# Gate and up by seven block products instead of eight (Strassen) in a mixed mLSTM and attention block

## The chip, the cores and the metric

The kernel runs on one core of a Trainium2 chip. The metric is the time of one execution on the device in microseconds (us), the median of several runs. All times below are of the kernel before the change, unless said otherwise.

## The reference, cut to what matters

```python
SEQ = 512
D_MODEL = 1024
D_FF = ((8 * D_MODEL + 3 * 256 - 1) // (3 * 256)) * 256          # 2816
...
        mod = jnp.dot(c_act, ada_w[l]) + ada_b[l]
        sh1, sc1, g1, sh2, sc2, g2 = jnp.split(mod, N_MOD, axis=-1)
...
        merged = (jax.nn.sigmoid(ga) * jnp.einsum('bsm,md->bsd', ym, p_mlstm[l])
                  + jax.nn.sigmoid(gb) * jnp.einsum('bsa,ad->bsd', ya, p_moba[l]))
        x = x + g1[:, None, :] * jnp.einsum('bsd,de->bse', merged, w_out[l])

        h = modulate(rms_norm(x, norm2_g[l]), sh2, sc2)
        f = jax.nn.silu(jnp.einsum('bsd,df->bsf', h, w_gate[l])) * jnp.einsum('bsd,df->bsf', h, w_up[l])
        x = x + g2[:, None, :] * jnp.einsum('bsf,fd->bsd', f, w_down[l])
    return rms_norm(x, normf_g)
```

All tensors are float32. The change touches the product of h (512 tokens x 1024) with w_gate and w_up (each 1024 x 2816); batch and depth are 1. ym and ya, the outputs of the mLSTM and of the attention, are computed ahead of what is shown.

## The kernel before, in words

**Products in float32.** Each float32 operand is held as two rounded parts, hi and lo. `mm3` (L220 to L223) makes one 128-deep product as three matmuls: hi by hi, hi by lo, lo by hi.

**Weights.** They come in 68 numbered blocks, the *chunks*, of mostly 1024 x 256 numbers (1 MB), kept in a buffer `raw` of four (`load`, L151). The attention and mLSTM input chunks come first, then C_P = 27 to 30 (merge projection), C_OUT = 31 to 34 (w_out), C_GU = 35 to 56 (w_gate and w_up in turn, 256 columns of D_FF each) and C_DN = 57 to 67 (w_down). `cvt(n, half)` turns half a chunk into hi (ACT, L204) and lo (DVE, L206), in `whl`. The chunks C_OUT and C_DN are first multiplied by the gate rows g1 or g2 on DVE (`gate_weights`, L176). `begin(n)` issues the load of a chunk two or three ahead and converts the first half of the next; `mid(n)` the second half.

**Gate and up.** Activations lie transposed: h2 is eight hi/lo pairs of 128 x 512 (128 of the 1024 features, 512 tokens). A unit is 128 columns of D_FF: eight steps of `mm3` on a chunk's 128 x 128 pieces (stationary) with h2 (512 columns, moving), so 24 matmuls of N = 512 a unit and 48 a chunk. `glu` takes silu of the gate unit on ACT (L1371) and multiplies by the up unit on DVE (L1372). The very first pair of chunks (`first`) runs in two halves of 256 tokens, since the second half of h2 is not there yet.

**Background jobs.** The rows of `mod` come from 24 jobs j, numbered over 256-column pieces of ada_w: an `ada` load of 1 MB in the buffers that the chunks use too, 15 operations on GpSimd (L271, L274), and a one-matmul `finish` (L743) with an addition on DVE (L745) that puts the piece into its row. Jobs 20 to 23 make g2. `rows_free` holds the jobs 20 to 23 back: they start once something has been appended to it. A recording layer with an estimated clock (`spend`, `pooled`) decides at build time where the pieces of a job stand between the other instructions; every engine then runs its own instructions in the order of that record.

**Queues.** All loads of chunks, of `ada` and of x are issued by SP, in one order. A load whose buffer is not free holds up those behind it.

Of the kernel before, what the change touches and what calls it, by code (L numbers as in the profile page):

```python
# [19 lines left out]
NT = 4  # L20
# [79 lines left out]
def block_kernel(ctx, tc, x, wall, adaw, pcol, prow, positions, inv_freq, out):  # L100
# [80 lines left out]
    def cvt(n, half, what=None, eng=None):  # L181
        if n >= len(KS):
            return
        if n not in parts:
            both = wp.tile([128, 2 * RAW], F32R, tag="whl", name=nm("whl"))
            parts[n] = (both[:, :SIZES[n]], both[:, SIZES[n]:2 * SIZES[n]])
        hi, lo = parts[n]
        if n == C_MV:
            dst = [t.rearrange("p (k n) -> p k n", k=8) for t in (hi, lo)]
            src = raws[n][:, :2048].rearrange("p (k n) -> p k n", k=8)  # L190
            ks = slice(half * 4, half * 4 + 4)
            cuts = [(src[:, ks, :], ks, slice(8, 264))]
# [27 lines left out]
    def mm3(o, lh, ll, rh, rl, start, stop):  # L220
        PE.matmul(o, lh, rh, start=start, stop=False)  # L221
        PE.matmul(o, lh, rl, start=False, stop=False)  # L222
        PE.matmul(o, ll, rh, start=False, stop=stop)  # L223
# [1074 lines left out]
    def h2_part(hf, qs):  # L1298
        for q in qs:
            pb = bank("a")  # L1300
            hq = T()
            for kk in range(2):
                k = 2 * q + kk
                for e in range(2):
                    PE.transpose(pb[:, kk * 256 + e * 128:kk * 256 + e * 128 + 128],
                                 nrm[2 * hf + e][k // 4][:, blk(k % 4)], ident[:])
            for kk in range(2):
                k = 2 * q + kk
                hm = hq[:, kk * 256:kk * 256 + 256]
                hi, lo = (h2[k][e][:, hf * 256:hf * 256 + 256] for e in range(2))  # L1310
# [84 lines left out]
    glu(bs[0], bs[2])
    glu(bs[1], bs[3])
    hT = h2
    rows_free.append(1)
    nfrow = []
# [7 lines left out]
    for ci in range(1, NF // 2):
        c = C_GU + 2 * ci
        cg = begin(c)
        pg = [None, None]  # L1410
        pg[0] = unit(cg, 0, bank("m"))
        mid(c)
        pg[1] = unit(cg, 1, bank("m"))
        cu = begin(c + 1)
        if ci == NF // 2 - 1:
            fps.update({k: fsplit(k) for k in range(2)})
        glu(pg[0], unit(cu, 0, bank("b")))
        mid(c + 1)
        glu(pg[1], unit(cu, 1, bank("b")))
        if ci == 4:  # L1420
            nfrow += [W(), W()]
            for q in range(2):
                SP.dma_start(nfrow[q][:, :512], flat(prow, PB + 2 * D + q * 512, [[0, 128], [1, 512]]))
# [146 lines left out]
```

## Time and profile before

| | us |
|---|---|
| median of three runs | 789.71 (789.25 to 789.99) |
| the profiled execution's own time | 789.44 |
| its span | 787.6 |
| TensorE matmul (PE) busy | 776.9, 99% |
| VectorE (DVE) busy | 416.4, 53% |
| ScalarE (ACT) busy | 311.4, 40% |

The span runs from the first to the last instruction of the profiled execution. An engine is busy while it works on at least one instruction; what follows is read by stages, since an average over the span hides which engine is the limit where. The stages of interest here: merge projection until 371.2 us, w_out until 416.5, the first gate and up pair until 441, the other 20 gate and up chunks until about 660, then w_down.

### The profile page before, as it was taken

Reading aid. Unit: us, or ns where it says so; the run is one execution under the profiler, and the core shown is the slowest. Engines: PE = TensorE matmul, PEld = TensorE weight load, DVE = VectorE, ACT = ScalarE, POOL = GpSimd, SP = SyncE. Lnnn points to the kernel's source line nnn. Section 1 sums busy time; section 2 is a strip of 40 time slices with the busy share of each in tenths; the row PEclk is TensorE's granted clock in tenths of the full one; section 3 lists DMA queues with packets and bytes.
Section 4 is the critical chain, followed back from the end, with each engine's and each line's share of the span. In section 5 each row is a group of like instructions: output and inputs, shape, how many; then the busy total and the mean of one; then the engine's idle time right before and its main releaser. Section 6 shows DMA issues by size and latency. Waiting matters only on the chain.

```text
span 787.6 us, 10146 instructions
## 1 busy us (share of the span) xinstructions
PE 776.9 (99%) x3891; PEld 642.3 (82%) x3891; DVE 416.4 (53%) x671; ACT 311.4 (40%) x541; POOL 299.5 (38%) x423
## 2 busy tenths in 40 slices
PE   8999999999999999999999999999999999999996
PEld 7789888778887787788889888888888888888885
DVE  4768687665565543478646333322322246555565
ACT  6679653324454454322356322221222113332243
POOL 5574436999866878950003695000000000000000
PEclk9999999999999999999999999999999999999999
DMA  9953325345431432345223425532232332222002
GB/s 326 387 195 142 107 80 174 120 150 205 155 108 54 161 107 107 134 187 183 102 90 108 154 74 200 213 108 75 86 107 108 107 108 88 76 104 107 0 1 107
DMA packets 22960, 102.49 MB, mean 130 GB/s; under 512 B 3448, under 2 KB 3584, under 8 KB 13312
## 3 DMA queue, kind: packets, MB, share of 16 engines
q1 hardware_dynamic: 21088, 99.43, 34.7%
q10 hardware_dynamic: 1824, 2.43, 1.1%
q8 instruction: 30, 0.49, 0.3%
q14 instruction: 18, 0.15, 0.1%
HBM read 97.65 MB, written 2.10 MB: 127 GB/s over the span
## 4 chain that ended last, share of the span: by engine, by line
PE 92%; DVE 3%; ACT 1%; DMA 1%; POOL 1%; issue 1%; POOLq 0%; ACTq 0%; DVEq 0%
PE psm L221 15%; PE psm L223 14%; PE psm L222 14%; PE psb L221 10%; PE psb L223 10%; PE psb L222 10%; PE psa L221 2%; PE psa L223 2%; PE psa L222 2%; PE psa L1091 1%; PE psc L1149 1%; PE psb L489 1%; PE psb L1132 1%; PE psa L591 1%; PE psm L591 1%
## 5 line engine op out<-in xcount | busy, mean ns | idle before, releaser
L206 DVE TENSOR_TENSOR whl<-raw,whl 128x1024 fp32r<-128x1024 f32 (+3 forms) x125 | 159.1, 1282 | 166.6 <-ACT whl L204 166.5
L204 ACT CAST whl<-raw 128x1024 fp32r<-128x1024 f32 (+2 forms) x124 | 127.2, 1045 | 276.0 <-PE psb L223 158.9
L1472 POOL TENSOR_TENSOR t<-x,v 128x512 f32<-128x512 f32 x1 | 1.3, 1297 | 288.4 <-DVE ss L1478 288.4
L274 POOL TENSOR_TENSOR accp<-accp,prod 128x256 f32<-128x256 f32 x112 | 90.2, 805 | 9.3
L221 PE MATMUL psb<-t,whl 128*128 128x512 f32 (+1 forms) x224 | 84.4, 377 | 0.0
L221 PE MATMUL psm<-t,whl 128*128 128x512 f32 (+1 forms) x224 | 84.3, 377 | 0.0
L223 PE MATMUL psm<-t,whl 128*128 128x512 f32 (+1 forms) x224 | 83.8, 374 | 0.0
L223 PE MATMUL psb<-t,whl 128*128 128x512 f32 (+1 forms) x224 | 83.8, 374 | 0.0
L222 PE MATMUL psm<-t,whl 128*128 128x512 f32 (+1 forms) x224 | 83.7, 374 | 0.0
L222 PE MATMUL psb<-t,whl 128*128 128x512 f32 (+1 forms) x224 | 83.7, 374 | 0.0
L221 PE MATMUL psm<-hh,whl 128*128 128x512 f32 x192 | 77.5, 404 | 0.4 <-ACT x L1073 0.4
L223 PE MATMUL psm<-hh,whl 128*128 128x512 f32 x192 | 75.0, 391 | 0.0
L222 PE MATMUL psm<-hl,whl 128*128 128x512 f32 x192 | 74.9, 390 | 0.0
L271 POOL TENSOR_SCALAR prod<-ada,cact 128x256 f32<-128x256 f32 x112 | 73.9, 660 | 0.0
L223 PEld LDWEIGHTS psm<-t,whl 128*128 128x128 f32 x224 | 42.2, 188 | 7.6
L223 PEld LDWEIGHTS psb<-t,whl 128*128 128x128 f32 x224 | 42.2, 188 | 7.6
L221 PEld LDWEIGHTS psm<-t,whl 128*128 128x128 f32 x224 | 42.2, 188 | 7.4
L222 PEld LDWEIGHTS psm<-t,whl 128*128 128x128 f32 x224 | 42.2, 188 | 7.4
L221 PEld LDWEIGHTS psb<-t,whl 128*128 128x128 f32 x224 | 42.2, 188 | 7.4
L222 PEld LDWEIGHTS psb<-t,whl 128*128 128x128 f32 x224 | 42.2, 188 | 7.4
L223 PEld LDWEIGHTS psm<-hh,whl 128*128 128x128 f32 x192 | 36.0, 188 | 8.2 <-DVE whl L206 0.4
L221 PEld LDWEIGHTS psm<-hh,whl 128*128 128x128 f32 x192 | 36.1, 188 | 8.1 <-ACT x L1073 0.7
(379 smaller groups left out, 1558.2 us busy)
## 6 DMA issues: line engine op xcount, KB each, us to landing
raw<-in_dram SPq DMA_DIRECT2D x59, 1024.0 KB, 4.8
ada<-in_dram SPq DMA_DIRECT2D x16, 1024.0 KB, 4.8
t<-in_dram SPq DMA_DIRECT2D x30, 256.0 KB, 6.1
raw<-in_dram SPq DMA_DIRECT2D x8, 448.0 KB, 6.6
xin<-in_dram SPq DMA_DIRECT2D x4, 512.0 KB, 5.0
v<-in_dram SPq DMA_DIRECT2D x8, 256.0 KB, 5.8
t<-t ACTq DMA_DIRECT2D x32, 64.0 KB, 2.1
x<-in_dram SPq DMA_DIRECT2D x8, 256.0 KB, 7.5
```

The lines of the kernel that those rows point to most:

```text
L204: (eng.tensor_copy if eng else A.copy)(hi[:, s], raws[n][:, s])
L206: (eng or V).tensor_tensor(out=lo[:, s], in0=raws[n][:, s], in1=hi[:, s].bitcast(F32), op=ALU.subtract)
L221: PE.matmul(o, lh, rh, start=start, stop=False)
L222: PE.matmul(o, lh, rl, start=False, stop=False)
L223: PE.matmul(o, ll, rh, start=False, stop=stop)
L271: G.tensor_scalar(t[:], rv[:, k, :], cact[:, k:k + 1], 1.0, op0=ALU.mult, op1=ALU.mult)
L274: G.tensor_tensor(out=p[:], in0=p[:], in1=t[:], op=ALU.add)
L489: PE.matmul(wb[:, :128], ident[:], ones, start=True, stop=True)
L591: PE.matmul(g1[m][:], w[:, blk(m)], h[:], start=k == 0 and e == 0, stop=k == KD - 1 and e == 2)
L1091: PE.matmul(bs[e][:, o:o + n], qp[a][r, blk(i)], kp[b][r, :n], start=g == 0, stop=g == 2)
L1132: PE.transpose(tb[:, o + (i - j) * 128:o + (i - j + 1) * 128], es[i][:, blk(j)], ident[:])
L1149: PE.matmul(yb[e * 64:e * 64 + 64, 128 * j:512], av[j][:, (2 * p + e) * 64:(2 * p + e + 1) * 64], t[j], start=j == 0, stop=j == NT - 1)
```

## The change

Chunks 35 and 36 are computed as before. Chunk 37 is computed in two halves of 256 tokens (`plain`). The 19 chunks 38 to 56 go through `seven`: a chunk's weights are cut in 2 x 2 blocks (512 features x 128 columns), h in 2 x 2 blocks (512 features x 256 tokens), and the four output blocks come from seven products of sums and differences (the form of Strassen's method with common sums, after Winograd) instead of eight. A product is 12 matmuls of N = 256, so a chunk has 84. The sums of h (`moving`) are made once. Those of the weights (`sums13`, `sums24`) are made for each chunk on DVE, in place in `raw`; each is rounded on ACT and its remainder made on DVE (`rounded`, `remainder`). Products 1, 6, 7 and 4 are added up in one PSUM region y, which ACT or DVE reads in between; 5 and 3 in z; 2 in x. Product 4 of a chunk runs after product 1 of the next one.

So that there is room in SBUF, the converted chunks lie in four single slots instead of two double ones, h2 is laid out otherwise, x (the residual, 2 MB) is written to DRAM before the stage and read again after it, and chunks of the merge stage are loaded two ahead rather than three. `rows_free` gets its entry in the merge stage (d == 1) instead of after the first `glu`.

```diff
@@ converted chunks, loads ahead @@
+    def slot():
+        return wp.tile([128, RAW], F32R, tag="whl", name=nm("whl"), bufs=4)
...
-            both = wp.tile([128, 2 * RAW], F32R, tag="whl", name=nm("whl"))
-            parts[n] = (both[:, :SIZES[n]], both[:, SIZES[n]:2 * SIZES[n]])
+            parts[n] = tuple(slot()[:, :SIZES[n]] for _ in range(2))
...
     def begin(n):
-        for e in range(2, 3 if C_MV <= n < C_P - 1 else 4):
+        for e in range(2, 3 if C_MV <= n < C_OUT else 4):
             load(n + e)
@@ merge stage @@
             split(pr[0][:], pr[1][:], ga)
+            if d == 1:
+                rows_free.append(1)
@@ gate and up @@
+    def moving():
+        b = {(r, c): [h2[c][2 * r + j][0] for j in range(2)] for r in range(2) for c in range(2)}
+        u1, u2, u3, u4 = ([H() for _ in range(2)] for _ in range(4))
+        mv.update({1: [p[1:] for p in h2[0][:2]], 2: [p[1:] for p in h2[0][2:]], 3: [p[1:] for p in h2[1][2:]]})
+        for n, o, x0, x1 in ((5, u1, b[0, 1], b[0, 0]), (6, u2, b[1, 1], u1), (7, u3, b[1, 1], b[0, 1]), (4, u4, b[1, 0], u2)):
+            for j in range(2):
+                V.tensor_tensor(out=o[j][:], in0=x0[j][:], in1=x1[j][:], op=ALU.subtract)
...
+    def sums13(n):
+        s1t[n] = T()
+        V.tensor_tensor(out=four(s1t[n]), in0=block(n, 1, 0), in1=block(n, 1, 1), op=ALU.add)
+        V.tensor_tensor(out=block(n, 1, 0), in0=block(n, 0, 0), in1=block(n, 1, 0), op=ALU.subtract)
+
+    def sums24(n):
+        V.tensor_tensor(out=block(n, 0, 0), in0=four(s1t[n]), in1=block(n, 0, 0), op=ALU.subtract)
+        V.tensor_tensor(out=block(n, 0, 1), in0=block(n, 0, 1), in1=block(n, 0, 0), op=ALU.subtract)
+
+    def make(n, products):
+        remainder(*rounded(n, products))
...
+        A.copy(hi, src)
...
+    def remainder(hi, lo, src):
+        V.tensor_tensor(out=lo, in0=src, in1=hi.bitcast(F32), op=ALU.subtract)
+
+    FIRST, LAST = C_GU + 3, C_DN - 1
...
+            mm3(o, wh[:, k, :], wl[:, k, :], hh, hl, k == 0 and p in (1, 2, 5), k == 3, True)
...
+    def late(n):
+        c = at[n]
+        if c["up"]:
+            f0, f1 = c["f"]
+            t0, c22 = c["late"]
+            V.tensor_tensor(out=f0[:], in0=f0[:], in1=t0[:], op=ALU.mult)
+            V.tensor_tensor(out=f1[:, 256:512], in0=f1[:, 256:512], in1=c22, op=ALU.mult)
+
+    def finish4(n):
+        product(n, 4)
+        c = at[n]
+        f = c["f"][1][:, 0:256]
+        if c["up"]:
+            V.tensor_tensor(out=f, in0=f, in1=c["y"], op=ALU.mult)
+        else:
+            A.activation(f, c["y"], AF.Silu)
+
+    def seven(n):
...
+        product(n, 1)
+        A.copy(m1, c["y"])
+        if n > FIRST:
+            finish4(n - 1)
+        elif more:
+            sums13(n + 1)
+        make(n, (7, 4))
+        load(n + 3)
...
+        product(n, 5)
+        A.copy(m5, c["z"])
+        if more:
+            make(n + 1, (5,))
+        product(n, 2)
+        V.tensor_tensor(out=t0[:, 0:256], in0=c["x"], in1=m1, op=ALU.add)
+        if n > FIRST:
+            late(n - 1)
+        if more:
+            make(n + 1, (1, 2))
+        else:
+            cvt(C_DN, 0)
+        product(n, 6)
+        A.copy(u2, c["y"])
+        if more:
+            sums24(n + 1)
+        product(n, 3)
+        if more:
+            six = rounded(n + 1, (6, 3))
+        V.tensor_tensor(out=t0[:, 256:512], in0=c["z"], in1=u2, op=ALU.add)
...
+        product(n, 7)
+        V.tensor_tensor(out=c22, in0=c["y"], in1=m5, op=ALU.add)
...
+        if n + 1 < LAST:
+            sums13(n + 2)
+        if more:
+            remainder(*six)
...
+    for n in range(FIRST, LAST + 1):
+        seven(n)
+    cvt(C_DN, 1)
+    fps[1] = fsplit(1)
+    finish4(LAST)
+    late(LAST)
```

SP's queue in the merge and w_out stages, before: job 19's load (ada_3563) is the last `ada` load; raw_3626, raw_3710, raw_3806, raw_3898 and raw_3960 are chunks 31 to 35, and the eight x loads (seven left out here) stand ahead of the last three.

```order
L264 DMA ada_3563<-in_dram 128x2048 [waits DMAHW0_49,Pool_49]
L159 DMA raw_3626<-in_dram 128x2048 [waits DMAHW6_49,DVE_49]
L159 DMA raw_3710<-in_dram 128x2048 [waits DMAHW7_49,DVE_49]
L1253 DMA x_3754<-in_dram 128x512 [waits PE_49]
...
L159 DMA raw_3806<-in_dram 128x2048 [waits DMAHW5_49,DVE_49]
L159 DMA raw_3898<-in_dram 128x2048 [waits DMAHW6_49,DVE_49]
L159 DMA raw_3960<-in_dram 128x2048 [waits DMAHW7_49,DVE_49]
```

The same place after: ada_3592, ada_3762, ada_3875 and ada_3983 are the loads of jobs 20 to 23, raw_3655 to raw_4066 chunks 30 to 35; v_3764 is a row of ada_b for g2.

```order
L267 DMA ada_3592<-in_dram 128x2048 [waits DMAHW5_49,Pool_49]
L163 DMA raw_3655<-in_dram 128x2048 [waits DMAHW7_49,Pool_49]
L163 DMA raw_3740<-in_dram 128x2048 [waits DMAHW6_49,DVE_49]
L267 DMA ada_3762<-in_dram 128x2048 [waits DMAHW1_49,Pool_49]
L777 DMA v_3764<-in_dram 128x512 [waits PE_49]
L1258 DMA x_3800<-in_dram 128x512
...
L163 DMA raw_3864<-in_dram 128x2048 [waits DMAHW6_49]
L267 DMA ada_3875<-in_dram 128x2048 [waits DMAHW7_49,Pool_49]
L163 DMA raw_3969<-in_dram 128x2048 [waits DMAHW0_49,DVE_49]
L163 DMA raw_3971<-in_dram 128x2048 [waits DMAHW7_49,DMAHW1_49,Pool_49]
L267 DMA ada_3983<-in_dram 128x2048 [waits DMAHW2_49,DVE_49]
```

The `ada` loads of jobs 20 to 23 have moved between the chunk loads of the w_out stage, and ada_3762, ada_3875 and raw_3971 wait on GpSimd (Pool), so whatever stands behind them in SP's queue waits for a job too.

DVE in the gate and up stage, before, one pair of chunks (whl: remainders of weights, 1024 elements a partition; f: the product with the gate unit).

```order
L206 TENSOR_TENSOR whl_5029<-raw_4907,whl_5029 128x1024
L1372 TENSOR_TENSOR f_5057<-f_5057,psb_5032 128x512
L206 TENSOR_TENSOR whl_5029<-raw_4907,whl_5029 128x1024
L1372 TENSOR_TENSOR f_5087<-f_5087,psb_5062 128x512
L206 TENSOR_TENSOR whl_5096<-raw_4970,whl_5096 128x1024 x2
```

The same engine after, one chunk (in the next one stand two further rows, the multiplications of `late`). L1453 are remainders, L1432 to L1437 sums of weights, L1515, L1529 and L1533 additions from PSUM, L1478 the last multiplication of the chunk before.

```order
L1453 TENSOR_TENSOR whl_5581<-t_5527,whl_5581 128x512
L1515 TENSOR_TENSOR t_5534<-psm_5533,v_5535 128x256
L1453 TENSOR_TENSOR whl_5597<-raw_5329,whl_5597 128x1024
L1436 TENSOR_TENSOR raw_5329<-t_5527,raw_5329 128x4x128
L1437 TENSOR_TENSOR raw_5329<-raw_5329 128x4x128
L1529 TENSOR_TENSOR t_5534<-psb_5532,x_5536 128x256
L1533 TENSOR_TENSOR x_5536<-psm_5531,v_5535 128x256
L1432 TENSOR_TENSOR t_5643<-raw_5446 128x512
L1433 TENSOR_TENSOR raw_5446<-raw_5446 128x4x128
L1453 TENSOR_TENSOR whl_5627<-raw_5329,whl_5627 128x1024
L1478 TENSOR_TENSOR hs_5414<-hs_5414,psm_5531 128x256
L1453 TENSOR_TENSOR whl_5680<-raw_5329,whl_5680 128x1024
```

Where a pair of chunks had six operations on DVE, it now has twenty-five: eleven a chunk, and three multiplications a pair (one of them the L1478 above).

## Rows read from the trace of the kernel before

**Rows 1.** The page: busy time of each engine; the chain that ended last.
```profile
PE 776.9 (99%) x3891; PEld 642.3 (82%) x3891; DVE 416.4 (53%) x671; ACT 311.4 (40%) x541; POOL 299.5 (38%) x423
...
PE 92%; DVE 3%; ACT 1%; DMA 1%; POOL 1%; issue 1%; POOLq 0%; ACTq 0%; DVEq 0%
```

**Rows 2.** Busy time by stage: w_out, first pair, most of the others.
```profile
core 0: us, PE busy (x) PEld busy (x) DVE busy (x) ACT busy (x) POOL busy (x), PEclk, DMA share, GB/s
371.20:416.50 45.30, 45.30 (x209) 37.68 (x208) 26.78 (x38) 19.85 (x35) 2.42 (x3) 1.00 0.27 94
416.50:441.00 24.50, 24.50 (x207) 24.46 (x206) 11.97 (x24) 15.98 (x28) 11.97 (x16) 1.00 0.24 86
441.00:650.00 209.00, 209.00 (x925) 173.05 (x925) 64.47 (x66) 46.84 (x56) 34.90 (x50) 1.00 0.35 126
```

**Rows 3.** Timeline of PE, gate and up: start, duration; 31 matmuls, first and last.
```profile
464.69 0.39 PE L223 MATMUL psm<-t,whl 128*128 128x512 f32 x1
...
471.49 0.39 PE L223 MATMUL psm<-t,whl 128*128 128x512 f32 x1
```

**Rows 4.** Timeline of PE, first pair: 49 matmuls of N = 256, first and last.
```profile
416.53 0.28 PE L221 MATMUL psm<-t,whl 128*128 128x256 f32 x1
...
422.29 0.28 PE L221 MATMUL psb<-t,whl 128*128 128x256 f32 x1
```

**Rows 5.** Timeline of DVE, gate and up; in brackets the idle time before.
```profile
525.08 0.69 DVE L1372 TENSOR_TENSOR f<-f,psb 128x512 f32<-128x512 f32 x1 [3.20 <-PE psb L223]
525.69 1.22 DVE L206 TENSOR_TENSOR whl<-raw,whl 128x1024 fp32r<-128x1024 f32 x1
...
531.54 2.36 DVE L206 TENSOR_TENSOR whl<-raw,whl 128x1024 fp32r<-128x1024 f32 x2 [0.32 <-ACT whl L204]
```

**Rows 6.** Groups of DVE by form: busy us, mean ns of one, idle before.
```profile
L198 DVE TENSOR_TENSOR whl<-raw,whl 128x1024 fp32r<-128x1024 f32 x2 | 2.4, 1222 | 1.3 <-ACT whl L196 1.3
...
L903 DVE TENSOR_TENSOR v<-psm,bt 128x256 f32<-128x256 f32 x4 | 1.7, 413 | 0.0
```

**Rows 7.** Groups of ACT by form, the same columns.
```profile
L204 ACT CAST whl<-raw 128x1024 fp32r<-128x1024 f32 x115 | 118.3, 1049 | 270.7 <-PE psb L223 158.9 <-PE psm L223 89.8 <-issue 7.7
...
L1371 ACT ACTIVATE f<-psm 128x512 f32<-128x512 f32 x16 | 9.4, 594 | 0.0
...
L303 ACT COPY t<-psc 128x256 f32<-128x256 f32 x3 | 1.1, 373 | 3.7 <-PE psc L301 3.7
```

**Rows 8.** Timeline of GpSimd: first and last operation of job 19.
```profile
332.68 0.49 POOL L271 TENSOR_SCALAR accp<-ada,cact 128x256 f32<-128x256 f32 x1
...
345.58 0.74 POOL L274 TENSOR_TENSOR accp<-accp,prod 128x256 f32<-128x256 f32 x1
```

**Rows 9.** The same of job 23, in gate and up.
```profile
477.08 0.69 POOL L271 TENSOR_SCALAR accp<-ada,cact 128x256 f32<-128x256 f32 x1 [4.24 <-DMA ada<-in_dram]
...
486.96 0.73 POOL L274 TENSOR_TENSOR accp<-accp,prod 128x256 f32<-128x256 f32 x1
```

**Rows 10.** SP, issue of chunks 33 and 34; DMA issues 344 to 357: KB, us to landing.
```profile
359.59 12.17 SPq L159 DMA_DIRECT2D raw<-in_dram  x2
...
raw<-in_dram SPq DMA_DIRECT2D x2, 1024.0 KB, 7.1
x<-in_dram SPq DMA_DIRECT2D x8, 256.0 KB, 7.5
ada<-in_dram SPq DMA_DIRECT2D x1, 1024.0 KB, 4.8
```

**Rows 11.** Timeline of PE: end of w_out; a finishing matmul and its neighbours.
```profile
400.43 0.39 PE L221 MATMUL psm<-whl,mh 128*128 128x512 f32 x1
...
471.71 0.59 PE L743 MATMUL psc<-accp,ones_r 128*128 128x256 f32 x2
471.96 0.58 PE L221 MATMUL psm<-t,whl 128*128 128x512 f32 x1
472.37 0.39 PE L222 MATMUL psm<-t,whl 128*128 128x512 f32 x1
```

More of the change, by code (lines that the diff above doesn't have):

```diff
@@ L111, in block_kernel @@
     sp = ctx.enter_context(tc.tile_pool(name="sp", bufs=4))
+    dp = ctx.enter_context(tc.tile_pool(name="dp", bufs=NT, space=bass.MemoryType.DRAM))
     ps = ctx.enter_context(tc.tile_pool(name="ps", bufs=2, space=bass.MemoryType.PSUM))
@@ L218, in mid, with mm3 @@
         cvt(n + 1, 1)
[L220 to L223, printed above, removed]
+    def mm3(o, lh, ll, rh, rl, start, stop, again=False):
+        PE.matmul(o, lh, rh, start=start, stop=False, skip_group_check=again)
+        PE.matmul(o, lh, rl, start=False, stop=False, skip_group_check=again)
+        PE.matmul(o, ll, rh, start=False, stop=stop, skip_group_check=again)
         spend(0.68 * max(rh.shape[-1], 270) / 512)
@@ L1253, in block_kernel, with H @@
                         SP.dma_start(xr[i][hf][:], x[blk(i), hf * 512:(hf + 1) * 512])
-    def hp2():
-        return (T(dt=F32R), T(dt=F32R))
-    h2 = [hp2() for _ in range(KD)]
+    h2 = [[None] * 4 for _ in range(2)]
+    def H(dt=F32):
+        return hp.tile([128, 512], dt, tag="h", name=nm("hs"))
     nrm = {}
@@ L1300, in h2_part @@
             pb = bank("a")
-            hq = T()
+            spare = H if hf else T
+            hq = spare()
+            keep = H if hf and q < 2 else T
+            h2[hf][q] = (hq, keep(dt=F32R), keep(dt=F32R))
             for kk in range(2):
@@ L1309, in h2_part @@
                 hm = hq[:, kk * 256:kk * 256 + 256]
-                hi, lo = (h2[k][e][:, hf * 256:hf * 256 + 256] for e in range(2))
+                hi, lo = (h2[hf][q][e][:, kk * 256:kk * 256 + 256] for e in (1, 2))
                 A.activation(hm, pb[:, kk * 256:kk * 256 + 256], AF.Identity, scale=modA[:, 8 + k:9 + k],
@@ L1362, in block_kernel @@
     normed2(2)
+    xkeep = [dp.tile([128, D], F32, tag="xk", name=nm("xk")) for _ in range(NT)]
     ft = []
@@ L1383, in first @@
                 ms = blk(q % 2)
-                mm3(bs[q][:, t], ch[0][:, k, ms], ch[1][:, k, ms], h2[k][0][:, t], h2[k][1][:, t], k == 0,
-                    k == KD - 1)
+                _, hh, hl = (v[:, k % 2 * 256:k % 2 * 256 + 256] for v in h2[hf][k // 2])
+                mm3(bs[q][:, t], ch[0][:, k, ms], ch[1][:, k, ms], hh, hl, k == 0, k == KD - 1)
+    mv = {}
+    def moving():
[5 more added lines that the diff above has]
+                V.tensor_tensor(out=o[j][:], in0=x0[j][:], in1=x1[j][:], op=ALU.subtract)
+            mv[n] = []
+            for j in range(2):
+                pr = (T(dt=F32R), T(dt=F32R))
+                split(pr[0][:], pr[1][:], o[j][:])
+                mv[n].append(pr)
+            yield
@@ new lines, in block, with both, four @@
+    def block(n, r, c):
+        return raws[n][:, :2048].rearrange("p (k n) -> p k n", k=8)[:, 4 * c:4 * c + 4, blk(r)]
+    def both(n, r):
+        return raws[n][:, :2048].rearrange("p (k n) -> p k n", k=8)[:, :, blk(r)]
+    stat, s1t = {}, {}
+    def four(t):
+        return t[:, :512].rearrange("p (k n) -> p k n", k=4)
+    def sums13(n):
+        s1t[n] = T()
+        V.tensor_tensor(out=four(s1t[n]), in0=block(n, 1, 0), in1=block(n, 1, 1), op=ALU.add)
+        V.tensor_tensor(out=block(n, 1, 0), in0=block(n, 0, 0), in1=block(n, 1, 0), op=ALU.subtract)
@@ new lines, in sums24, with rounded @@
+    def sums24(n):
[3 more added lines that the diff above has]
+        remainder(*rounded(n, products))
+    def rounded(n, products):
+        t = slot()
+        w = 4 * len(products)
+        hi, lo = (t[:, e * 1024:e * 1024 + 128 * w].rearrange("p (k n) -> p k n", n=128) for e in range(2))
+        src = four(s1t[n]) if products == (5,) else both(n, 0 if products in ((1, 2), (6, 3)) else 1)
+        A.copy(hi, src)
+        for e, p in enumerate(products):
+            stat[n, p] = (hi[:, 4 * e:4 * e + 4, :], lo[:, 4 * e:4 * e + 4, :])
+        return hi, lo, src
@@ new lines, in remainder, with product @@
+    def remainder(hi, lo, src):
+        V.tensor_tensor(out=lo, in0=src, in1=hi.bitcast(F32), op=ALU.subtract)
+    FIRST, LAST = C_GU + 3, C_DN - 1
+    at = {}
+    def product(n, p):
+        o = at[n][{2: "x", 5: "z", 3: "z"}.get(p, "y")]
+        wh, wl = stat.pop((n, p))
+        for k in range(4):
+            hh, hl = (v[:, k % 2 * 256:k % 2 * 256 + 256] for v in mv[p][k // 2])
+            mm3(o, wh[:, k, :], wl[:, k, :], hh, hl, k == 0 and p in (1, 2, 5), k == 3, True)
[6 more added lines that the diff above has]
+            V.tensor_tensor(out=f1[:, 256:512], in0=f1[:, 256:512], in1=c22, op=ALU.mult)
@@ new lines, in finish4 @@
+    def finish4(n):
[7 more added lines that the diff above has]
+    def seven(n):
+        up = (n - C_GU) % 2
+        c = at[n] = {"up": up}
+        for r, t in zip("yzx", "mbm" if up else "aaa"):
+            c[r] = bank(t)[:, 0:256]
+        if up:
+            c["f"] = at[n - 1]["f"]
+            t0 = T()
+        else:
+            c["f"] = [H() if len(ft) + e < 16 else X() for e in range(2)]
+            ft.extend(c["f"])
+            t0 = c["f"][0]
+        f0, f1 = c["f"]
+        ta, tb = W(), X()
+        m1, m5, u2 = ta[:, 0:256], ta[:, 256:512], tb[:, 0:256]
+        c22 = tb[:, 256:512] if up else f1[:, 256:512]
+        more = n < LAST
+        product(n, 1)
[6 more added lines that the diff above has]
+        load(n + 3)
+        if not more:
+            gate_weights(C_DN, 0)
+            fps[0] = fsplit(0)
+        product(n, 5)
[8 more added lines that the diff above has]
+            make(n + 1, (1, 2))
+        else:
+            cvt(C_DN, 0)
[7 more added lines that the diff above has]
+        V.tensor_tensor(out=t0[:, 256:512], in0=c["z"], in1=u2, op=ALU.add)
+        if not up:
+            A.activation(f0[:], t0[:], AF.Silu)
+        product(n, 7)
+        V.tensor_tensor(out=c22, in0=c["y"], in1=m5, op=ALU.add)
+        if up:
+            c["late"] = (t0, c22)
+        else:
+            A.activation(c22, c22, AF.Silu)
+        if n + 1 < LAST:
+            sums13(n + 2)
+        if more:
+            remainder(*six)
@@ L1387, in block_kernel, with plain @@
+    def plain(n, m, pb):
+        wh, wl = parts_of(n)
+        for hf in range(2):
+            t = slice(hf * 256, hf * 256 + 256)
+            for k in range(KD):
+                _, hh, hl = (v[:, k % 2 * 256:k % 2 * 256 + 256] for v in h2[hf][k // 2])
+                mm3(pb[:, t], wh[:, k, blk(m)], wl[:, k, blk(m)], hh, hl, k == 0, k == KD - 1)
     first(0, (0, 1))
     first(0, (2,))
+    sums13(FIRST)
     h2_part(1, (0, 1, 2))
@@ L1391, in block_kernel @@
     h2_part(1, (3,))
+    mk = moving()
+    next(mk)
     first(1, (0, 1))
-    cvt(C_GU + 2, None)
-    first(1, (2, 3))
[L1395 to L1399, printed above, removed]
+    cvt(C_GU + 2, 0)
+    next(mk)
+    cvt(C_GU + 2, 1)
+    for b in bs[:2]:
+        ft.append(H())
+        A.activation(ft[-1][:], b[:], AF.Silu)
+    first(1, (2, 3))
+    for f, b in zip(ft, bs[2:]):
+        V.tensor_tensor(out=f[:], in0=f[:], in1=b[:], op=ALU.mult)
+    make(FIRST, (5,))
+    make(FIRST, (1, 2))
+    load(FIRST + 2)
+    at[FIRST - 1] = {"f": [H() for _ in range(2)]}
+    ft.extend(at[FIRST - 1]["f"])
+    pgs = [bank("a"), bank("a")]
+    plain(FIRST - 1, 0, pgs[0])
+    A.activation(ft[2][:], pgs[0][:], AF.Silu)
+    next(mk)
+    next(mk)
+    sums24(FIRST)
+    plain(FIRST - 1, 1, pgs[1])
+    A.activation(ft[3][:], pgs[1][:], AF.Silu)
+    make(FIRST, (6, 3))
+    for i in range(NT):
+        for q in range(2):
+            SP.dma_start(xkeep[i][:, q * 512:q * 512 + 512], xr[i][q][:])
     fps = {}
@@ L1405, in fsplit @@
         return pr
[L1407 to L1423, printed above, removed]
+    for n in range(FIRST, LAST + 1):
[4 more added lines that the diff above has]
+    late(LAST)
+    nfrow = [T(), T()]
+    for q in range(2):
+        SP.dma_start(nfrow[q][:, :512], flat(prow, PB + 2 * D + q * 512, [[0, 128], [1, 512]]))
+    for i in range(NT):
+        for q in range(2):
+            xr[i][q] = T()
+            SP.dma_start(xr[i][q][:], xkeep[i][:, q * 512:q * 512 + 512])
     while bg[0]:
```

2 lines of the change are left out of this document (1 added, 1 removed).

## The prediction

> **What bounds the kernel now.** I read the page first. PE is busy 776.9 of 787.6 us and makes 92% of the chain that ended last [rows 1]: the reader is to see that nothing but fewer or shorter PE instructions gains, and that any gap made in PE's row is lost in full. Then the windows by stage: in w_out, in the first pair and in gate and up, PE's busy time equals the length of the stage, at a granted clock of 1.00, the upper level of 2.4 GHz [rows 2]. DVE works 26.78 of 45.3 us in w_out (59%) and 64.47 of 209 in gate and up (31%); there is free time on DVE where the change puts work, and less where it moves GpSimd's jobs. Last the timelines, for the price of one matmul of each width.
>
> **What the products save.** With N = 512, matmuls start 30 intervals apart from 464.69 to 471.49: 226.7 ns each [rows 3]. With N = 256, 48 intervals from 416.53 to 422.29: 120.0 ns, the change of bank at the end included [rows 4]. A chunk took 48 x 0.2267 = 10.88 us and now takes 84 x 0.120 = 10.08: 0.80 less, not an eighth, since half the width costs 53% of the time. Nineteen chunks: **-15.2**. Chunk 37 has 96 x 0.120 = 11.52 for 10.88: **+0.6**.
>
> A rule speaks against narrow matmuls. First the rows: in the first pair, half of which is of N = 256, PEld is busy 24.46 of 24.50 us with 206 loads, 119 ns each [rows 2], so weight loads fill their lane, but starts stay at 120.0 ns. The Trainium skill, TensorE: Matmul & The Clock Gate, section Back-to-back issue gap, says that in a stream of load and matmul both set the spacing, and gives about 81 ns for N = 128 and 131 for N = 512. On a straight line between (an estimate from that page) N = 256 would be some 98 ns, and seven products dearer than eight: 84 x 98 = 8.2 against 48 x 131 = 6.3 us. The trace disagrees at both widths, 226.7 and 120.0, and the sum goes by the trace.
>
> **What is added to DVE, ACT and the loads in gate and up.** DVE operations in a row overlap a little: two of 1024 take 2.36 us (1.14 for the one more; 1.22 alone), and after one of 512 the next starts 0.61 later (0.69 alone) [rows 5]. One of 256 takes 0.41 alone [rows 6]; less the same 0.07, 0.34. A chunk has three of 1024 (remainders), five of 512 (a remainder, four sums) and three of 256 (additions): 3.42 + 3.05 + 1.02 = 7.49. A pair adds three multiplications (0.61 + 2 x 0.34): 16.27 us, against PE's 20.16, 81%. The sums read the weights with a stride; L198, a strided remainder, takes 1222 ns like a plain one [rows 5, 6], so the stride costs nothing. ACT: three roundings of 1024 and one of 512 (1.05, about 0.6), three copies of 0.37 from PSUM, and in gate chunks three silus (0.59, 2 x 0.37) [rows 7]: 4.9 and 6.2 us a chunk, under 62%. Loads: one of 1 MB, 4.8 us [rows 10], per 10.08; the eight of x (7.5) are wanted only after the down products.
>
> So no engine but PE is full. Whether PE waits is a question of order. I laid a chunk's DVE rows behind the ends of its products (1.44 us each): remainders of products 7 and 4 are done at 5.3 (wanted at 8.64), of the next chunk's 1 and 2 at 8.5 (10.08), of its 6 and 3 at 13.0 (15.84). The tightest is the addition that reads y behind product 7: done at 10.7, and product 4 wants y at 11.52, 0.8 later. Hence 0 here; that slack is the cover, and the second rival is what happens without it.
>
> **What moves: GpSimd's jobs 20 to 23.** Before, they ran beside the first gate and up chunks, where nobody waited. Now their loads stand among the loads of w_out's chunks, and each waits for GpSimd to let a buffer go. The chain: job 19 ends at 345.58 + 0.74 = 346.3 [rows 8]. Job 20 follows. Job 21's load is issued at job 20's last read of a buffer, 0.74 before its end, and takes 4.8 to land [rows 10]: 4.06 between jobs, three times. Job 23's load stands behind chunk 34's, issued by the same wait, and a second 1 MB lands at 7.1 instead of 4.8 [rows 10]: 2.3. So job 23 ends at 346.3 + 4L + 12.2 + 2.3 = 360.8 + 4L, with L the length of a job.
>
> L lies between 10.6 (477.08 to 487.69, DVE busy 31% in that stage) [rows 9] and 13.6 (332.68 to 346.32) [rows 8]. DVE's share in w_out, 59%, lies between; I take the middle, 12.1. Then the last job ends at 409.2. PE must run that job's finishing matmul in the last quarter of w_out, among matmuls that before ran at 400.43; three earlier finishes add 0.43 each (from 471.49 to 472.37 is 0.88, less two regular spacings) [rows 3, 11]: 401.7. PE's queue stands until the job is done, every matmul behind it too: **+7.5** (1.5 at 10.6; 13.5 at 13.6). What hid this before is that the jobs lay later; DVE's gating of chunks 33 and 34, loaded together at 359.59 before [rows 10] and now behind two jobs, is late by a like amount and is contained in the same wait.
>
> On L, the Trainium skill, SBUF - State Buffer, section Who interferes with whom, says that DVE and GpSimd share a pair of ports, which one of them holds exclusively. By that, jobs beside w_out's DVE work would be long ones, 13.6 like job 19's, and the sum +0.4 (the third rival); by the rows that I take, -5.6. The trace agrees in direction alone, 13.6 against 10.6.
>
> **Ends of the stage.** At its start the sums for the first chunk and the four differences of h come among DVE's work of the first pair, half idle there (11.97 of 24.5) [rows 2]: between 0 and 1, **+0.3**. At its end product 4 of the last chunk follows product 7 at once, waits for the addition (0.41, and its start), and the first down products then wait for a multiplication behind a remainder of 1.22 on DVE: 0 to 2, **+1.2**.
>
> **Sum.** -15.2 + 0.6 + 7.5 + 0.3 + 1.2 = -5.6, on the profiled execution's 789.44: 783.8. The median stands 0.27 above it: **784.1**.
>
> **The rivals.**
> - *The jobs are in time.* L of 10.6 throughout, since a standing PE leaves DVE idle too: the wait is 1.5, the sum -11.6, **778.1**. For it: job 23 did run so. Against: w_out keeps DVE at 59%.
> - *DVE becomes the bound* (the other side). If its operations don't overlap (1.22, 0.69, 0.41) a pair costs 18.2 us; with some 2 us a chunk of waiting for ACT's rounding or for PE ahead of an operation, 22.2, against 20.16: 1.0 a chunk, +19, **803**. It decides from a loss of 0.3 us a chunk on (5.6 / 19). For it: the order is rigid, one late addition holds the sums behind it. Against: remainders waited but 0.32 for ACT [rows 5], and I found 0.8 of slack.
> - *Jobs as long as job 19*, 13.6 each: the wait is 13.5, the sum +0.4, **790.1**, no change. For it: job 19 ran beside the same stage of the program. Against: it had a busier DVE.
> - *Weight loads bound narrow matmuls*, so that the seven products save nothing: if 119 ns a load [rows 2] grew by a tenth, without overlap left, a chunk would take 84 x 0.131 = 11.0, 0.12 more than before instead of 0.80 less, the sum +11.9 and **802**. The page of TensorE stands behind this one. Against: 48 even intervals [rows 4].
>
> **How the numbers follow.** The forecast has 0.55, with a range of its own of 780 to 788 (L from 11.2 to 13.1); jobs in time 0.17; DVE as the bound 0.13; jobs of full length 0.13; weight loads 0.02. A measurement tells 0.2%, 1.6 us, from no change. Faster, below 788.1: forecast and first rival, 0.72. Same: the third rival, mostly, 0.13. Slower: 0.15. From 777 to 790.5 the range leaves out the two slow cases and the tails of the others, near 0.2.
>
> **What would show it.** Right: matmuls of N = 256 at 120.0 ns through gate and up, a chunk every 10.08 us; DVE near 80% and ACT near 55% there; one or more gaps in PE between 371 and about 420, some 7 in sum, ended by GpSimd's accp, by DVE's gated weights or by a DMA; the four jobs back to back with 4 us between. Wrong: gaps in each chunk's row of products, ended by DVE (second rival); no gap in w_out (first); spacing off 120.0.

## The result and the profile after

The changed kernel takes 793.57 us (median of four, 793.37 to 794.77) against 789.62: a ratio of 1.0053, interval 1.0036 to 1.0071. That is 0.5% slower, beyond the bound of 0.2%, where 784.1 was forecast and 0.72 given to faster. The profiled execution has a span of 791.9 us, 4.3 more than before.

First the page of the kernel after: busy time and the chain that ended last, as in [rows 1].

```profile
PE 767.8 (97%) x4623; PEld 666.9 (84%) x4623; DVE 533.3 (67%) x869; ACT 368.7 (47%) x654; POOL 309.7 (39%) x423
...
PE 73%; POOL 13%; DMA 5%; DVE 4%; ACT 2%; issue 2%; SPq 0%; POOLq 0%; DVEq 0%; ACTq 0%
```

PE is busy 9 us less than before, yet the span grew: the chain, which ran over PE for 92% of the span, runs over it for 73% and goes over GpSimd (13%) and DMA (5%) as well. The windows of the same stages (columns as in [rows 2]) say where.

```profile
371.20:416.50 45.30, 34.33 (x137) 26.31 (x135) 25.16 (x28) 12.23 (x19) 33.11 (x37) 0.89 0.36 139
416.50:441.00 24.50, 22.76 (x119) 19.59 (x120) 11.89 (x24) 12.98 (x27) 4.73 (x7) 0.93 0.55 215
441.00:650.00 209.00, 209.00 (x1746) 209.00 (x1745) 176.65 (x264) 113.20 (x182) 3.30 (x4) 1.00 0.31 107
```

Up to 441 us the engine stands, 11 us of it in w_out, at a granted clock below 1; in gate and up it is full, 1746 matmuls in 209.0 us, 119.7 ns each, with DVE at 85%. The loss lies before the new products, not in them.

The timeline of PE after, at the ends of the stages: the first matmul of gate and up, the 49th, and the first of w_down. Before, the first of these was at 416.53 [rows 4].

```profile
436.54 0.28 PE L224 MATMUL psm<-t,whl 128*128 128x256 f32 x1
...
442.30 0.28 PE L224 MATMUL psb<-t,whl 128*128 128x256 f32 x1
...
665.11 0.40 PE L224 MATMUL psa<-whl,t 128*128 128x512 f32 x1
```

And the first of w_down in the timeline of the kernel before:

```profile
660.81 0.39 PE L221 MATMUL psa<-whl,t 128*128 128x512 f32 x1
```

So gate and up (the first pair included) begins 20.0 us late, takes 228.57 instead of 244.28 us (15.7 less), and from there on both kernels need 126.8: 20.0 - 15.7 = 4.3.

Where the 20.0 come from: who waited for whom on PE, longest first (us in total, times, longest).

```profile
PE psm L224 <- DVE t L1246: 7.5, 1, 7.5
PE psc L746 <- POOL accp L277: 3.9, 1, 3.9
...
PE psm L225 <- DVE whl L209: 1.3, 3, 0.8
```

The first is the start of w_out. DVE's row says why DVE was late itself: it stood 10.5 us for chunk 32, whose gating is in its queue ahead of the multiplications that w_out waits for; and SP issued that chunk late. DVE's row first:

```profile
376.92 1.23 DVE L180 TENSOR_TENSOR raw<-raw,t 128x1024 f32<-128x1024 f32 x1 [10.51 <-DMA raw<-in_dram]
```

SP's timeline (issues):

```profile
361.92 0.33 SPq L267 DMA_DIRECT2D ada<-in_dram  x1
...
362.78 6.17 SPq L1258 DMA_DIRECT2D x<-in_dram  x8
369.29 0.33 SPq L163 DMA_DIRECT2D raw<-in_dram  x1
```

Job 21's load went out at 361.92, when job 20 let its buffer go. Behind it the eight loads of x took 6.17 us of SP's queue, and chunk 32's load went out at 369.29. The timeline of GpSimd has the four jobs (first operation of each, and the last of all):

```profile
346.42 1.98 POOL L274 TENSOR_SCALAR accp<-ada,cact 128x256 f32<-128x256 f32 x1
...
366.91 0.48 POOL L274 TENSOR_SCALAR accp<-ada,cact 128x256 f32<-128x256 f32 x1 [4.19 <-DMA ada<-in_dram]
...
380.44 0.48 POOL L274 TENSOR_SCALAR accp<-ada,cact 128x256 f32<-128x256 f32 x1 [4.17 <-DMA ada<-in_dram]
...
404.64 0.48 POOL L274 TENSOR_SCALAR accp<-ada,cact 128x256 f32<-128x256 f32 x1 [6.61 <-DMA ada<-in_dram]
...
417.46 0.72 POOL L277 TENSOR_TENSOR accp<-accp,prod 128x256 f32<-128x256 f32 x1
```

The gaps for the loads are 4.2, 4.2 and 6.6. The lengths, from each start to where the idle time before the next begins, are 16.3, 9.4, 17.6 and 13.5 (the last to 418.2). The short one, job 21, ran while DVE stood (from 366.4 to 376.9). The finishing matmul of job 23 starts with its end:

```profile
418.24 1.05 PE L746 MATMUL psc<-accp,ones_r 128*128 128x256 f32 x2 [3.88 <-POOL accp L277]
```

Last the clock: two windows of 4 us at the end of the first wait and behind it, then the second wait and the work behind it (the column after the count of POOL is the granted clock).

```profile
376.00:380.00 4.00, 0.52 (x1) 0.50 (x2) 3.05 (x4) 0.00 (x0) 0.28 (x1) 0.50 0.85 313
380.00:384.00 4.00, 3.83 (x10) 2.48 (x9) 3.08 (x6) 1.57 (x2) 3.44 (x4) 0.50 0.50 213
...
414.20:418.20 4.00, 0.16 (x1) 0.00 (x0) 0.00 (x0) 0.00 (x0) 3.74 (x7) 1.00 0.00 0
...
419.00:421.60 2.60, 2.60 (x7) 2.01 (x6) 1.11 (x2) 0.27 (x1) 0.00 (x0) 0.50 0.92 369
```

At the end of the 7.5 us without a matmul the grant is at 0.50, the level of 1.2 GHz, and the first ten matmuls of w_out run at it. Through the second wait, of 3.9, it stays at 1.00, but just behind it is at 0.50 as well, and the next seven matmuls run at that.

The sum of the 20.0: job 23 is finished at 418.24 instead of the 401.7 that PE would have needed, 16.5; four finishing matmuls that before came later, 4 x 0.43 = 1.7; and the half clock behind the last wait, from 418.24 to 421.99 where 2.02 are needed, 1.7. Together 19.9. The first wait and its half clock lie inside the 16.5: by this sum PE would without them have stood that much longer at the last job.

### The profile page after: what moved, and what is told of

Same layout as the page of the kernel before. It is cut to its first block, busy times and chain, and to the rows that moved or that the text cites. A ratio compares the mean times of both kernels' runs of the same rounds, so it can differ in the third digit from the quotient of the medians.

```text
span 791.9 us, 12027 instructions
## 1 busy us (share of the span) xinstructions
PE 767.8 (97%) x4623; PEld 666.9 (84%) x4623; DVE 533.3 (67%) x869; ACT 368.7 (47%) x654; POOL 309.7 (39%) x423
## 4 chain that ended last, share of the span: by engine, by line
PE 73%; POOL 13%; DMA 5%; DVE 4%; ACT 2%; issue 2%; SPq 0%; POOLq 0%; DVEq 0%; ACTq 0%
PE psm L224 10%; PE psm L226 10%; PE psm L225 10%; PE psa L225 6%; PE psa L226 6%; PE psa L224 6%; POOL prod L274 6%; POOL accp L277 5%; PE psb L224 5%; PE psb L226 5%; PE psb L225 5%; DMA ada<-in_dram 2%; DMA t<-in_dram 1%; PE psa L1094 1%; DVE t L656 1%
## 5 line engine op out<-in xcount | busy, mean ns | idle before, releaser
L209 DVE TENSOR_TENSOR whl<-raw,whl 128x1024 fp32r<-128x1024 f32 (+2 forms) x88 | 111.8, 1274 | 76.9 <-ACT whl L207 76.7
L207 ACT CAST whl<-raw 128x1024 fp32r<-128x1024 f32 (+2 forms) x87 | 88.5, 1034 | 104.9 <-PE psb L225 67.7
L1447 ACT CAST whl<-raw 128x1024 fp32r<-128x1024 f32 x57 | 59.8, 1049 | 61.0 <-DVE raw L1437 40.8
L1453 DVE TENSOR_TENSOR whl<-raw,whl 128x1024 fp32r<-128x1024 f32 x57 | 69.7, 1222 | 24.4 <-ACT whl L1447 24.3
L274 POOL TENSOR_SCALAR prod<-ada,cact 128x256 f32<-128x256 f32 x112 | 84.1, 751 | 0.0
L224 PE MATMUL psa<-t,whl 128*128 128x256 f32 x276 | 78.1, 283 | 0.0
L225 PE MATMUL psa<-t,whl 128*128 128x256 f32 x276 | 78.1, 283 | 0.0
L226 PE MATMUL psa<-t,whl 128*128 128x256 f32 x276 | 78.1, 283 | 0.0
L224 PE MATMUL psm<-t,whl 128*128 128x256 f32 (+1 forms) x256 | 76.2, 298 | 0.5 <-DVE x L1533 0.5
L226 PE MATMUL psm<-t,whl 128*128 128x256 f32 (+1 forms) x256 | 75.8, 296 | 0.0
L225 PE MATMUL psm<-t,whl 128*128 128x256 f32 (+1 forms) x256 | 75.8, 296 | 0.0
L224 PEld LDWEIGHTS psa<-t,whl 128*128 128x128 f32 x276 | 53.0, 192 | 0.0
L225 PEld LDWEIGHTS psa<-t,whl 128*128 128x128 f32 x276 | 53.0, 192 | 0.0
L226 PEld LDWEIGHTS psa<-t,whl 128*128 128x128 f32 x276 | 53.0, 192 | 0.0
L224 PEld LDWEIGHTS psm<-t,whl 128*128 128x128 f32 x256 | 49.0, 191 | 2.0 <-DVE x L1533 0.7
L226 PEld LDWEIGHTS psm<-t,whl 128*128 128x128 f32 x256 | 49.0, 191 | 1.3
L225 PEld LDWEIGHTS psm<-t,whl 128*128 128x128 f32 x256 | 49.0, 191 | 1.2
```

Source lines behind the costliest of these rows:

```text
L224: PE.matmul(o, lh, rh, start=start, stop=False, skip_group_check=again)
L225: PE.matmul(o, lh, rl, start=False, stop=False, skip_group_check=again)
L226: PE.matmul(o, ll, rh, start=False, stop=stop, skip_group_check=again)
L274: G.tensor_scalar(t[:], rv[:, k, :], cact[:, k:k + 1], 1.0, op0=ALU.mult, op1=ALU.mult)
```

## Experiments

**The theory** that I set out to test: the 20 us are waits for jobs 20 to 23, which run in series with their loads and with the chunks that share buffers and SP's queue with them, and the products bring what was forecast. Rivals: the shorter prefetch, the loads by themselves, or DVE as the bound of the new products.

**Without the four jobs.** From the changed kernel; g2 keeps only its bias part.

```diff
-            if j < 23:
+            if j < 19:
                 ada_load(j + 1)
...
+            if j >= 20:
+                continue
```

> The changed kernel with the four background jobs of the g2 row left out (no loads, no GpSimd work, no finishing matmuls; the g2 row stays at its bias part, so the output is not the reference's). Theory (the 20 us lost ahead of gate and up are waits for these jobs, in series through SP's queue and GpSimd, and the half clock behind the waits): w_out runs without a gap, gate and up begins at about 416.5 us as before, the stage of products takes 228 to 229 us as now, total about 773.5. Rival (chunks loaded two ahead instead of three, and single slots for converted chunks, make w_out late even without the jobs): gaps stay in w_out, total 780 or more.

774.24 us, a ratio of 0.9806 (0.9792 to 0.9821). The window of w_out of this run, columns as in [rows 2], shows no gap:

```profile
371.20:416.50 45.30, 45.30 (x210) 37.69 (x210) 27.07 (x38) 19.85 (x35) 2.38 (x3) 1.00 0.29 96
```

The rival of the shorter prefetch, and of the single slots with it, falls: with both in place w_out is as before.

**The move alone.** The kernel before, with the one line moved.

```diff
             split(pr[0][:], pr[1][:], ga)
+            if d == 1:
+                rows_free.append(1)
...
-    rows_free.append(1)
```

> The kernel before with the one line on rows_free moved into the merge stage (d == 1), nothing else; chunks are loaded three ahead as before. Theory (the chain of jobs alone sets the end of w_out: job, load, job, load): the finishing matmul of the last job still waits until about 413 to 418 us, loss of 14 to 19 us, total 804 to 808. Rival (the shorter prefetch of the changed kernel is what lets a job hold up a chunk, so that the move alone is nearly free): total below 795.

813.98 us against 789.41, 1.0306 (1.0289 to 1.0323): 24.6 slower, beyond the 14 to 19 of the theory. With the longer prefetch a chunk's load stands ahead of job 20's, which goes out at 345.63 instead of 332.02; job 20 starts 4 us later (350.51 instead of 346.42), and more of PE's waits are for chunks:

```profile
PE psm L221 <- ACT whl L204: 4.7, 2, 4.1
PE psc L743 <- POOL accp L274: 4.5, 2, 3.9
PE psm L221 <- DVE x L1280: 3.2, 1, 3.2
...
PE psm L222 <- DVE whl L206: 1.8, 3, 0.9
```

So the move costs by itself more than the whole loss of the changed kernel. That the shorter prefetch eased it there fits these starts, but was not tried by itself: the slots for converted chunks differ too. The theory had the place right and the size, again, too small.

**Jobs of one product.** All loads, waits and finishing matmuls in place, GpSimd computes only the first of the eight products of each job, so the g2 row is incomplete.

```diff
         for k in range(8):
+            if k and j >= 20:
+                pooled(1.4)
+                yield
+                continue
```

> The changed kernel with all loads, waits and finishing matmuls of jobs 20 to 23 in their places, but GpSimd computes only the first of the eight products of each (fifteen operations become one; output not the reference's). Theory (the length of a job, L, is what is wrong in the sum): with L of 0.5 the last job ends near 363 to 365 us, no wait in w_out, total about 775.3 (the four finishing matmuls at 0.43 are still there). Rival (the ada loads between the chunk loads on SP's queue are late by themselves): a gap of some us stays in w_out, total over 779.

776.01 us, 0.9829 (0.9809 to 0.9848). No wait is left in w_out. It is 1.8 above the run without jobs, the four finishing matmuls (1.7). The loads cost nothing of their own; in this arrangement of buffers and queues the length of the jobs is what counts.

**The last finishing matmul later.**

```diff
-            if (force or clock[0] > max(ready + 7.0, c_last[0] + 5.0)) and not c_taken:
+            if (force or clock[0] > max(ready + (7.0 if j < 23 else 25.0), c_last[0] + 5.0)) and not c_taken:
```

> The changed kernel, the finishing matmul of job 23 recorded later by 18 us of the recording clock, which puts it into gate and up; the jobs themselves stay. Theory: only the second wait (4.0 us) and the half clock behind it (some 1.5) go, the first wait of 7.5 and its half clock stay: total about 788. Rival (the job chain has a second taker: the chunk loads behind ada of job 23 wait as long, and the wait comes back elsewhere): total 792 or more.

787.77 us, 0.9978 (0.9967 to 0.9988): 5.8 less than the changed kernel, which is the second wait (from 414.19, where the next matmul was due, to 418.24: 4.05) and the 1.7 of half clock behind it. Nothing came back elsewhere. The first wait stayed, at 7.2.

**Products on ScalarE.**

```diff
-            G.tensor_scalar(t[:], rv[:, k, :], cact[:, k:k + 1], 1.0, op0=ALU.mult, op1=ALU.mult)
+            if j < 20:
+                G.tensor_scalar(t[:], rv[:, k, :], cact[:, k:k + 1], 1.0, op0=ALU.mult, op1=ALU.mult)
+            else:
+                A.activation(t[:], rv[:, k, :], AF.Copy, scale=cact[:, k:k + 1])
```

> The changed kernel, the eight products of a job 20 to 23 on ScalarE instead of GpSimd, which keeps the seven sums. Theory (the length of a job on GpSimd, stretched beside DVE, is the cause): seven sums of 0.74 are 5.2 us alone and some 8 beside DVE; with the same gaps for the loads the last job ends at about 346.4 + 32 + 15 = 393, before PE comes to it: total 776 to 779. Rival (the wait only changes its engine): ScalarE's products stand in its queue ahead of the roundings of weights and wait there for the ada loads, 4.8 us each: gaps in PE's row ended by ScalarE's whl, total 783 or more.

782.02 us, 0.9906 (0.9886 to 0.9925), between the two. Both long waits are gone, but the rival is half right: PE waits 1.6 us for ScalarE's roundings of weights and 2.4 for DVE's remainders, some of them right behind these. ScalarE's timeline of this run has a product waiting for its load, and a rounding of weights behind it:

```profile
391.48 0.51 ACT L277 ACTIVATE accp<-ada,cact 128x256 f32<-128x256 f32 x1 [4.68 <-DMA ada<-in_dram]
391.89 1.03 ACT L207 CAST whl<-raw 128x1024 fp32r<-128x1024 f32 x1
```

**Buffers of their own.** Jobs 21 to 23 are loaded into tiles of the general pool by `ada_fetch`, which the first jobs use already; the last finishing matmul later as above.

```diff
+        rv = araw[j] if j > 20 else [araw[j][:, k * 256:k * 256 + 256] for k in range(8)]
...
-                ada_load(j + 1)
+                (ada_fetch if j >= 20 else ada_load)(j + 1)
```

> The changed kernel, jobs 21 to 23 loaded into four free tiles each of the general pool instead of a chunk buffer (the finishing matmul of job 23 later, as in the run before). The length of the jobs stays. Theory (jobs in series with their loads, since job, next load and next chunks share buffers): the gaps of 4 to 6 us between jobs go, the last job ends near 346.4 + 4 x 15 = 406, nobody waits for it; chunk 32 waits for job 20's buffer and chunks 33 and 34 stand behind job 22's pieces, some 3 to 5 us of wait in all: total 779 to 782. Rival (GpSimd's length alone counts): the last jobs and what stands behind them are as late as before, total 786 or more.

779.86 us, 0.9878 (0.9851 to 0.9905), from two executions that lie apart, 781.71 (the profiled one) and 778.02: as expected in size, but by another wait. PE stood 3.5 us for the end of job 22 at its finishing matmul (396.33), which the recording clock had put too early; PE's list of waits has none for the gated chunks, where 3 to 5 us were expected.

**The jobs' true price.** As before, and:

```diff
-            pooled(0.65)
+            pooled(0.65 if j < 20 else 1.1)
...
-                pooled(0.75)
+                pooled(0.75 if j < 20 else 1.0)
+            if k == 5 and 20 < j < 23:
+                ada_fetch(j + 1)
...
-            if j < 23:
+            if j < 21:
```

> As the run with own buffers, and the recording clock counts a job with 16 us instead of 11.2 (the measured lengths are 16.3 and 17.6 beside a busy DVE), and job j + 1's pieces are fetched behind two thirds of job j: so chunks 33 and 34 stand ahead of job 22's pieces on SP's queue, and all finishing matmuls come later. Theory: only chunk 32's wait for job 20's buffer is left (about 1 us, half of it covered): total 776 to 778, that is the run with one product a job (776.0) or little more. Rival (a longer GpSimd time beside gate and up hurts DVE there, and PE with it): total over 781.

By this edit the price of a job goes from 10.45 us (8 x 0.65 + 7 x 0.75) to 15.8, where the expectation has 11.2 and 16.

776.08 us against 789.46, 0.9830 (0.9814 to 0.9847): 13.4 faster than before and 17.5 faster than the change as made, with all of the jobs' work in place. Its window of w_out:

```profile
371.20:416.50 45.30, 45.03 (x207) 36.94 (x206) 29.94 (x40) 19.72 (x35) 33.60 (x35) 1.00 0.41 143
```

The first operations of its jobs 20 to 23, from GpSimd's timeline:

```profile
346.20 1.98 POOL L274 TENSOR_SCALAR accp<-ada,cact 128x256 f32<-128x256 f32 x1
...
362.49 0.48 POOL L274 TENSOR_SCALAR accp<-t,cact 128x256 f32<-128x256 f32 x1
...
377.31 2.51 POOL L274 TENSOR_SCALAR accp<-t,cact 128x256 f32<-128x256 f32 x1
...
395.58 0.48 POOL L274 TENSOR_SCALAR accp<-t,cact 128x256 f32<-128x256 f32 x1
```

Jobs 20 to 22 are as long as ever (16.3, 14.8, 18.3, back to back) and in the same place. Job 23's last two products now run at the start of gate and up and end at 420.81, later than the 418.2 of the changed kernel; yet PE waits 0.3 us in w_out. What cost some 17 us was not that the jobs lay there, but that chunks and PE's queue were tied to them. In steps: 5.8 for the last finishing matmul, 7.9 for the buffers, 3.8 for the higher price and the earlier fetch, which were not tried apart.

**One more remainder in each chunk**, in the run without jobs.

```diff
-            make(n + 1, (1, 2))
+            r12 = rounded(n + 1, (1, 2))
+            remainder(*r12)
+            remainder(*r12)
```

> The run without the four jobs (774.2), and in each of the 18 chunks the remainder of products 1 and 2 is computed twice (one more DVE operation of 1024, 1.14 us a chunk). This measures how near DVE is to being the bound of the stage of products. Theory (0.8 us of slack at the tightest place, DVE at 81 to 85%): DVE has 18.6 of 20.2 us a pair, PE waits 0 to 0.4 us a chunk: total 774 to 781. Rival (DVE is as good as the bound already, waits on ScalarE included): all of the 1.14 shows in each chunk, total 793 or more.

783.52 us, 9.3 more than the 774.24, 0.5 a chunk: beyond the theory's 0 to 0.4 (774 to 781 in all), far from the rival's 1.14. The waits on PE are where the prediction saw the least slack, at the addition behind product 7 (L1537 in this run):

```profile
PE psa L224 <- DVE hs L1537: 1.8, 6, 0.4
PE psm L224 <- DVE x L1537: 1.2, 2, 0.7
PE psa L224 <- DVE x L1537: 0.9, 3, 0.3
```

The list leaves out short waits. In PE's timeline the first matmul of product 4 starts some 0.45 us late behind most gate chunks and 0.23 behind most up chunks, and the second 0.10 late each time: 8.9 of the 9.3. From 1.14 added and 0.55 or 0.33 lost, the slack there is an estimated 0.6 us in gate chunks and 0.8 in up chunks, where 0.8 was worked out. DVE is not the bound, but it has room for only about that much more in each chunk.

**Remainders off DVE.** From the run with the true price; for chunks 28 to 34 the second part of the weights is a copy on ScalarE in place of the remainder, so the products are not those of the reference.

```diff
-        if what != "hi":
+        if C_P < n < C_GU:
+            A.copy(lo[:, s], raws[n][:, s])
+        elif what != "hi":
```

> The run with own buffers and the true price (776.1), and for chunks 28 to 34 the second part of the weights is a copy made on ScalarE instead of the remainder on DVE (it has the wrong value, so the output is not the reference's): 14 operations of 1.22 us with both inputs in SBUF leave DVE while jobs 20 to 23 run. Nobody waits for the jobs here, so their lengths can be read by themselves: 16.3, 14.8, 18.3 for jobs 20 to 22 there. Theory (DVE's operations stretch GpSimd's): they fall to 10.6 to 14. Rival (the length comes from the transfers beside, or is a matter of chance): 15 to 18 as before. The total stays within 3 us of 776 either way, unless ScalarE becomes late.

775.8 us in one execution. Jobs 20 to 22 start at 343.02, 355.32 and 368.35, job 23 at 383.10: 12.3, 13.0 and 14.8 instead of 16.3, 14.8 and 18.3; job 19 took 11.0 instead of 13.6. All four (19 to 22) are shorter with fewer DVE operations beside them, jobs 20 and 21 within the range of the theory, job 22 just above it. The loads are the same ones, though jobs 20 to 22 start 3 to 9 us earlier beside them. So part of a job's length is DVE's doing; how it divides between operations was not tried.

## Why the prediction was wrong

**The products** were right. Chunks of 84 x 0.120, chunk 37, and the end of the stage make -15.2 + 0.6 + 0.5, with the finishing matmuls that left the stage (-1.7) -15.8; measured -15.7. The start cost nothing (0.3 forecast), the end 0.52 (1.2). Their matmuls took 119.7 ns each over the stage, with PEld busy throughout. The estimate from the sustained figures of the Trainium skill (TensorE: Matmul & The Clock Gate, Back-to-back issue gap), by which narrow matmuls would have been dearer, does not hold for these.

**DVE as the bound** (the rival on the other side) did not occur: 85% busy, 81 forecast, no wait of PE but the one at the end. A loss on that side came, but by the third rival's mechanism.

**The step that failed is the wait for the jobs**, "**+7.5**", and in it its length L: "DVE's share in w_out, 59%, lies between; I take the middle, 12.1". The chain was right in most links: jobs in series, 15.0 us of gaps (14.5 forecast), PE standing at the last finishing matmul, a late chunk inside the same wait. That chunk was not one of 33 and 34, as forecast, but chunk 32, and its wait came at the start of w_out. But the four lengths sum to 56.8, 14.2 each, outside the bounds of 10.6 and 13.6 that I took from two jobs: the formula, with 56.8 and 15.0, gives 346.3 + 71.8 = 418.1, and 418.2 was measured. That is 9.0 us later than 409.2.

The step between the bounds went by DVE's share of busy time, and that does not order the jobs. The windows of job 19 before, and of jobs 22 and 23 after (DVE's busy time is the third of the five):

```profile
332.68:346.32 13.64, 13.64 (x64) 11.37 (x63) 10.43 (x15) 4.29 (x6) 13.05 (x16) 1.00 0.22 78
...
380.44:398.03 17.59, 17.42 (x69) 13.74 (x68) 13.34 (x14) 4.90 (x6) 17.00 (x15) 0.89 0.09 38
404.64:418.20 13.56, 8.61 (x35) 6.03 (x33) 6.29 (x7) 6.26 (x11) 12.96 (x15) 1.00 0.00 0
```

Job 23 took as long as job 19 with DVE busy 46% of the time instead of 76%, and job 22 took 4 us longer than job 19 at the same 76%. What does order them is the time in DVE operations with both inputs in SBUF, summed from DVE's timeline rows: 7.2 us beside job 19, and 10.4, 0, 11.6 and 4.8 beside jobs 20 to 23, which took 16.3, 9.4, 17.6 and 13.5. Beside jobs 20 and 22 stood the gating of weights, two and three operations of it. The run with remainders off DVE points the same way; that this kind of operation is the whole cause is not shown.

**A term was missing**: the clock. The sum let PE stand and go on at full speed. Behind the last wait seven matmuls ran at the lower level, 1.7 us (the 2.3 us lost in the same way behind the first wait lie inside the 16.5).

Put together: 7.5 became 16.5, 1.7 for the clock, less 1.0 at the ends of the stage: 784.1 + 9.0 + 1.7 - 1.0 = 793.8, against 793.57.

## What to carry to other kernels

A job in the background was free here only once no queue was tied to it: ask which buffer it shares, what stands behind its loads, and where its last matmul stands, before asking how long it takes. Price such jobs in the recording clock by their length beside the engines that will be busy there; here 15.8 us in place of 10.45, and the fetch moved with it, made the difference between 779.9 (two executions, 778.0 and 781.7) and 776.1. And where a stage gets faster at the cost of moving work out of it, time the work at its new place alone: the move by itself cost 24.6 us.

## What the runs showed of the hardware

GpSimd's operations of 0.48 us took up to 2.6 beside DVE operations with both inputs in SBUF. The timeline of the kernel after has such a case. GpSimd:

```profile
359.39 2.50 POOL L274 TENSOR_SCALAR prod<-ada,cact 128x256 f32<-128x256 f32 x1
```

DVE at the same time:

```profile
358.85 1.64 DVE L209 TENSOR_TENSOR whl<-raw,whl 128x1024 fp32r<-128x1024 f32 x1
360.41 1.21 DVE L180 TENSOR_TENSOR raw<-raw,t 128x1024 f32<-128x1024 f32 x1
```

The GpSimd operation lasts until both of DVE's are over, and DVE's first takes 1.64 instead of 1.22. The Trainium skill (SBUF — State Buffer, Who interferes with whom) says that a DVE operation with two inputs in SBUF contends with GpSimd's reads; the trace agrees, with 2.50 us for 0.48, and the run with remainders off DVE shows the jobs shortened by 2 to 4 us. I had named that page and given its outcome as a rival, at the length of job 19; two of the four real lengths were beyond it.

The granted clock was at 0.50 behind waits of 7.5 and 3.9 us, for some 4.8 and 3.4 us of work. In the first wait it fell while PE stood; through the second it was 1.00, and it fell only after the matmuls had begun again, at about 418.5.
